# Cached loads and broadcast queries issued by GpSimd, and fourteen matmuls of ones ahead of the first transposition

## The chip, the cores and the metric

The kernel runs on one core of a Trainium2 chip. The metric is the device time of one execution in microseconds. Before the change three runs took 1572.55, 1575.05 and 1578.77 us; their median is 1575.05 us.

The engines are named as the profile names them: PE is TensorE (PEld its weight loads), DVE is VectorE, ACT is ScalarE, POOL is GpSimd, SP is SyncE. SP computes nothing here and issues transfers. "SPq" and "ACTq" are the instructions with which SP and ACT issue them.

## The reference

One inference step of a small decoder with two layers, for a prompt of 512 tokens and for 8 sequences of 8 new tokens each. Layer 0 is attention, layer 1 a state-space layer; each is followed by a gated feed-forward layer. Only the attention of the 8 sequences touches the caches, and the change lies there:

```
DIL_GROUPS = ((128, 1), (512, 4), (2048, 16))        # window, dilation
q = rope(rmsnorm(qkv[:, :, 0], q_gain), pos); k = rope(rmsnorm(qkv[:, :, 1], k_gain), pos); v = qkv[:, :, 2]
for g, (win, dil) in enumerate(DIL_GROUPS):
    kv_all = concatenate([bufs[g], kv_new], axis=1)   # cache, then the new rows
    o, l = dilated_block(q[:, :, g], kv_all, qi, dil, win // dil + 1)
wts = softmax(stack(lses)); o = einsum('gbqh,gbqhd->bqhd', wts, stack(outs))
```

A query of group g sees the cached keys at distances 0, d, 2d, up to the window, 129 keys in each group. The eight new tokens of a sequence together need 1, 4 and 8 sets ("units") of 128 cached rows in the three groups. A unit of keys or of values is 128 rows of 512 fp32 numbers, 256 KB. The caches are also outputs, shifted by 8 rows. All arithmetic is fp32; large matmuls are done as three products of parts rounded to fp32r (`mm6`, and L351 to L353).

## The kernel before

**Order of work.** `_build` (L51) runs in this order: the projections (`qkv_phase`, L417), the attention (`attn_phase`, L596), the output projection (`wo_phase`, L737), the first feed-forward layer with the setup of the state-space layer as filling, the state-space layer, the second feed-forward layer. The Tile framework takes this program with a list of dependences, lets buffers rotate in pools, and puts each engine's instructions into an order with its own model of time (`schedule_with_timeline_sim=True`, L1354). At run time each engine, SP and its transfers included, works through its list in that order and waits where an instruction is not ready.

**The start.** `Tokens.__init__` (L234) issues the first loads: the identity matrix (ACT's queue, L246), the norm gains `gr` (L247 and L253), and in turn a quarter of the prompt `xn` (L250) and a piece of the first weight (L255, by `fetch_w`, L85). The first PE instruction transposes `gr` into a PSUM tile `ps` (L260), and DVE copies the result to `gm` (L261). The prompt's transpositions (`prompt`, L263, PE at L272) are placed after L260 by `issue_after` in `prep` (L311), and their results are scaled by `gm` on ACT (L274). `ones` is a constant of 128x128 that DVE fills at L62; before the change only `Norm.finish` (L196) multiplies with it.

**The projections.** `qkv_chunk` (L330) makes 512 columns of queries, keys or values of one group, 24 prompt and 4 sample matmuls for each of four weight pieces of 512 KB, which ACT and DVE split into `whi` (L99) and `wlo` (L100). The order of the nine chunks is: group 2 (window 2048) queries, keys, values, then queries and keys of groups 1 and 0, then values of groups 1 and 0 last.

**The cached keys** are worked in between. After each weight piece `step` (L502) looks in `PLAN`, a table written by hand, for what is to be traced at this place.
- Groups 1 and 0: `score` (L466). GpSimd clears and fills `Qz` (L471 to L479), `cache_tile` (L385) loads two units of keys into a `kc` buffer, PE transposes them (L488) and multiplies (L492).
- Group 2: `products` (L392). A load of two units of keys (L388) and a load of two queries, broadcast over 128 partitions from a DRAM scratch `qscr` (L396), both into `kc` buffers; they are multiplied (L397) and summed by DVE (L399). For six sequences this happens in the projections with DVE as multiplier and the pool `kst`, for the last two in the attention with GpSimd as multiplier and a pool `kpa` of four buffers. `close2` (L402) ends a sequence; GpSimd clears its `P` (L461 or L726) first.

**The attention.** `attn_phase` runs four head pairs of the prompt (`prompt_pair`, L621; its values `vt` were loaded at L592) and the eight sequences (`decode`, L668), two of them around each pair. A decode loads the new rows' values `vn` (L694) and 13 units of cached values in seven loads by `cache_tile` (L700) into the same `kst` pool of six `kc` buffers, and multiplies them (L704).

**Queues.** All cached loads (L388) and the broadcast queries (L396) are issued by SP, in one list with the weights (L87), the shifted copies of the caches (`pace`, L78, 80 of about 1 MB and 8 of 480 KB), `vn`, `vt` and the rest. ACT's queue has the outputs of new keys and values and the scratch stores. GpSimd issues no transfer.

Of the kernel before, what the change touches and what calls it, by code (L numbers as in the profile page):

```python
# [29 lines left out]
WIN = (128, 512, 2048)  # L30
# [10 lines left out]
def dram(ap, off, dims):  # L41
    return bass.AP(tensor=ap.tensor, offset=ap.offset + off, ap=[list(d) for d in dims])
# [190 lines left out]
class Tokens:  # L233
    def __init__(self, nc, A, L, kst, ptp, small, dk, xr):  # L234
        self.nc, self.L, self.ptp, self.small, self.kst, self.dk, self.xr = nc, L, ptp, small, kst, dk, xr
        c1 = L["c1"]
        self.h = c1.tile([128, KT, T], F32R, name="xh")
        self.l = c1.tile([128, KT, T], F32R, name="xl")
        self.s = c1.tile([128, KT, 128], F32R, name="xsp")
        self.ss = c1.tile([128, 4, 5], F32, name="ss")  # L240
        nc.vector.memset(self.ss, 1.0)
        self.raw, self.mark = [], {}
        ident, gm = L["ident"], L["gm"]
        gr = small.tile([32, 128], F32, name="gr")
        self.w = []
        nc.scalar.dma_start(ident, A["c_ident"])  # L246
        nc.sync.dma_start(gr[0:16], A["norm_mix"].rearrange("l (k p) -> (l k) p", p=128))  # L247
        for i in range(4):
            xn = kst.tile([128, 4, 256], F32, name="kc")
            nc.sync.dma_start(xn, dram(A["x_prompt"], i * 256, [[4 * D, 128], [D, 4], [1, 256]]))  # L250
            self.raw.append(xn)
            if i == 0:
                nc.scalar.dma_start(gr[16:32], A["norm_ffn"].rearrange("l (k p) -> (l k) p", p=128))  # L253
                nc.scalar.activation(self.ss[:, 0, 0:1], self.ss[:, 0, 0:1], AF.Copy)
            self.w.append(L["fetch_w"](A["w_qkv"], 4608, i * 2, 2, 2 * 512, 512, 0.0))  # L255
            if i == 0:
                self.rs = kst.tile([64, D], F32, name="kc")
                nc.sync.dma_start(self.rs, A["x_sample"].rearrange("b j d -> (b j) d"))
        ps = L["psd"].tile([128, 136], F32, name="Sd")
        self.first = nc.tensor.transpose(ps[:, :32], gr, ident[:32, :32])  # L260
        self.gmc = nc.vector.tensor_copy(gm.rearrange("p (l m) k -> p m l k", m=2), ps[:, :32].rearrange("p (m l k) -> p m l k", m=2, l=2))  # L261

# [117 lines left out]
CACHES = ("cache_kv_w128", "cache_kv_w512", "cache_kv_w2048")  # L380
# [4 lines left out]
def cache_tile(nc, A, pool_, name, gi, b, c0, n, kv):  # L385
    t = pool_.tile([128, 2, 512], F32, name=name)[:, :n]
    st = STRIDE[gi]
    nc.sync.dma_start(t, dram(A[CACHES[gi]], (b * WIN[gi] + c0) * 1024 + kv * 512, [[st * 1024, 128], [1024, n], [1, 512]]))  # L388
    return t


def products(nc, A, L, eng, kst, P, b, part):  # L392
    c0 = 2 * part
    kc = cache_tile(nc, A, kst, "kc", 2, b, c0, 2, 0)
    qb = kst.tile([128, 2, 512], F32, name="kc")
    nc.sync.dma_start(qb, dram(L["qscr"], (b * 8 + c0) * 512, [[0, 128], [512, 2], [1, 512]]))  # L396
    eng.tensor_tensor(kc, kc, qb, OP.mult)  # L397
    for c in range(2):
        nc.vector.tensor_reduce(P[:, :, 0:2, c0 + c], kc[:, c].rearrange("p (a h d) -> p a h d", a=4, h=2), AX.X, OP.add)  # L399
# [17 lines left out]
def qkv_phase(nc, tc, A, es, L):  # L417
# [40 lines left out]
    def score2(b, part):  # L458
        if part == 0:
            prods[b] = dk.tile([128, 4, 4, 8], F32, name="P2", bufs=1)  # L460
            g.memset(prods[b], 0.0)  # L461
        products(nc, A, L, v, kst, prods[b], b, part)
        if part == 3:
            close2(nc, L, dk, psd, "Sd", prods.pop(b), b)

    def score(gi, b):  # L466
# [14 lines left out]
        for c0 in range(0, n, 2):  # L481
            w = min(2, n - c0)
            kc = cache_tile(nc, A, kst, "kc", gi, b, c0, w, 0)
            for c in range(w):
                u = c0 + c
                kp = ptp.tile([128, 4, 128], F32, name="pt")
                for hp in range(4):
                    te.transpose(kp[:, hp, :], kc[:, c, hp * 128:(hp + 1) * 128], ident)  # L488
                ks = dk.tile([128, 4, 128], F32, name="ks")
                s.activation(ks, kp, AF.Copy)  # L490
                for hp in range(4):
                    te.matmul(Sd[hp * 32:hp * 32 + 32, 0:128], Q[:, u, hp, :], ks[:, hp, :], start=u == 0, stop=u == n - 1,  # L492
                              tile_position=(0, hp * 32), skip_group_check=True)
# [102 lines left out]
def attn_phase(nc, tc, A, es, L):  # L596
# [71 lines left out]
    def decode(b):  # L668
# [28 lines left out]
        for gi in (0, 1, 2):  # L697
            for c0 in range(0, UNITS[gi], 2):
                w = min(2, UNITS[gi] - c0)
                vc = cache_tile(nc, A, kst, "kc", gi, b, c0, w, 1)  # L700
                for c in range(w):
                    for hp in range(4):
                        pz = pa[:, hp, :] if u == 0 else Z[:, u - 1, hp, :]
                        te.matmul(O[hp * 32:hp * 32 + 32, :], pz, vc[:, c, hp * 128:hp * 128 + 128], start=u == 0, stop=False, tile_position=(0, hp * 32), skip_group_check=True)  # L704
                    u += 1
# [14 lines left out]
    def score2():  # L720
        if not rest:
            return
        b, part = rest.pop(0)
        if part == 0:
            prods[b] = dk.tile([128, 4, 4, 8], F32, name="P2", bufs=1)
            g.memset(prods[b], 0.0)  # L726
        products(nc, A, L, g, kp, prods[b], b, part)
        if part == 3:
            close2(nc, L, dk, pD, "Sd", prods.pop(b), b)
# [628 lines left out]
```

## Time and profile before

| | |
|---|---|
| median of three runs | 1575.05 us |
| the profiled execution's own time | 1576.93 us |
| its span, first to last instruction | 1575.1 us |
| mean granted clock of PE | 0.978 |
| busy: PE, DVE, ACT, POOL | 1518.4, 925.1, 519.2, 304.1 us |
| cached loads, issued by SP | 96 of 512 KB, 16 of 256 KB |
| broadcast queries, issued by SP | 32 of 512 KB |
| moved by SP's queue | 304.81 MB |
| moved by ACT's queue | 18.04 MB |

The views used below are: the page with the busy time of each engine; the busy time by stretch (columns: from and to in us, length, then for each engine busy us and number of instructions, the granted clock of PE as a share of full speed, the mean busy share of the 16 DMA engines, and GB/s); the waits (who waited for whom: us in total, times, longest); and the order of time (start, duration, engine, line, operation, tiles written and read, and in brackets how long the engine stood before it and what released it). A row with x4 joins four instructions that follow each other. A view of one source line gives shortest, median and longest duration in ns. The chain of waits goes back from the last instruction to what released it.

The projections last until about 303 us, the attention until 463, the output projection starts at 465; from 480 us on the feed-forward and state-space layers follow.

### The profile page before, as it was taken

The page shows a single profiled execution, that of the slowest core. Times are in us where ns is not written, and L with a number is a line of the kernel's source. Part 1 is how long each engine was busy: PE and PEld are TensorE (multiplying, and loading weights), DVE is VectorE, ACT ScalarE, POOL GpSimd, SP SyncE. Part 2 cuts the span into 40 slices and gives each one's busy share as a digit, 9 for nine tenths or more (in the row PEclk, how much of TensorE's full clock was granted, in tenths as well). Part 3 has the DMA queues.
Part 4 walks back from the last instruction along what each step waited for, and adds up shares of the span by engine and source line. Part 5 has one row for each costly group of instructions (what it writes and reads, how often), then busy time and mean ns, then how long its engine had stood idle before and what let it go on. Part 6 is the DMA issues. An engine that isn't in the chain of part 4 may idle for free.

```text
span 1575.1 us, 28895 instructions
## 1 busy us (share of the span) xinstructions
PE 1518.4 (96%) x12010; PEld 1404.5 (89%) x12010; DVE 925.1 (59%) x1665; ACT 519.2 (33%) x774; POOL 304.1 (19%) x339
## 2 busy tenths in 40 slices
PE   8989999769989999999999999999999999999998
PEld 6868877546669999999999999999999999999998
DVE  5898954458637864388879667755353333333332
ACT  4433444424425222222222254333242212221222
POOL 2000111213003013745335430021011001100100
PEclk9999999879999999999999999899999999999999
DMA  8496248896786656589666765855555555443212
GB/s 274 164 345 216 98 132 273 285 346 232 250 281 169 224 187 220 186 293 315 212 236 241 242 225 180 273 163 195 189 186 203 209 186 212 144 142 95 81 61 81
DMA packets 193219, 324.69 MB, mean 206 GB/s; under 512 B 39488, under 2 KB 137024, under 8 KB 191552
## 3 DMA queue, kind: packets, MB, share of 16 engines
q1 hardware_dynamic: 183584, 304.81, 56.7%
q10 hardware_dynamic: 9504, 18.04, 3.3%
q8 instruction: 94, 1.54, 0.4%
q14 instruction: 37, 0.30, 0.1%
HBM read 290.27 MB, written 119.83 MB: 260 GB/s over the span
## 4 chain that ended last, share of the span: by engine, by line
PE 52%; DVE 2%; DMA 1%; issue 0%; ACT 0%; ACTq 0%; DVEq 0%
PE acc L106 48%; DMA u_scr<-uP 1%; PE aux L106 1%; DVE cb L1052 1%; DVE kk L1061 1%; PE acc L1180 0%; PE acc L1181 0%; PE acc L1142 0%; PE aux L1181 0%; PE aux L1045 0%; PE aux L1180 0%; DMA U<-u_scr 0%; PE aux L1056 0%; DVE Z L1162 0%; PE aux L818 0%
## 5 line engine op out<-in xcount | busy, mean ns | idle before, releaser
L100 DVE TENSOR_TENSOR wlo<-raw,whi 128x1024 fp32r<-128x1024 f32 x200 | 246.3, 1232 | 263.0 <-ACT whi L99 256.5
L99 ACT ACTIVATE whi<-raw 128x1024 fp32r<-128x1024 f32 x200 | 208.4, 1042 | 518.9 <-PE acc L106 403.1
L106 PE MATMUL acc<-xgl,whi 128*128 128x288 f32 x1760 | 378.6, 296 | 0.0
L106 PE MATMUL acc<-xgh,wlo 128*128 128x288 f32 x1760 | 377.7, 296 | 0.0
L106 PE MATMUL acc<-xgh,whi 128*128 128x288 f32 x1760 | 377.0, 296 | 0.1
L106 PEld LDWEIGHTS acc<-xgl,whi 128*128 128x128 f32 x1760 | 282.6, 188 | 1.2 <-issue 1.0
L106 PEld LDWEIGHTS acc<-xgh,wlo 128*128 128x128 f32 x1760 | 282.7, 188 | 0.6 <-issue 0.2
L106 PEld LDWEIGHTS acc<-xgh,whi 128*128 128x128 f32 x1760 | 281.7, 188 | 0.5 <-DVE gt L795 0.3
L797 POOL TENSOR_TENSOR gt<-gt,rstd 128x576 f32<-128x576 f32 x44 | 77.2, 1755 | 431.4 <-ACT gt L796 431.3
L106 PE MATMUL acc<-hh,whi 128*128 128x288 f32 x704 | 151.4, 296 | 0.0
L106 PE MATMUL acc<-hh,wlo 128*128 128x288 f32 x704 | 151.3, 296 | 0.0
L106 PE MATMUL acc<-hl,whi 128*128 128x288 f32 x704 | 151.1, 295 | 0.0
L352 PE MATMUL acc<-wlo,xh 128*128 128x512 f32 x288 | 114.4, 398 | 4.9 <-DVE wlo L100 4.8
L106 PEld LDWEIGHTS acc<-hh,wlo 128*128 128x128 f32 x704 | 113.1, 188 | 0.2 <-issue 0.2
L106 PEld LDWEIGHTS acc<-hl,whi 128*128 128x128 f32 x704 | 113.1, 188 | 0.2 <-issue 0.2
L106 PEld LDWEIGHTS acc<-hh,whi 128*128 128x128 f32 x704 | 113.2, 188 | 0.0
L353 PE MATMUL acc<-whi,xl 128*128 128x512 f32 x288 | 110.5, 394 | 0.0
L351 PE MATMUL acc<-whi,xh 128*128 128x512 f32 x288 | 106.7, 402 | 1.0 <-ACT whi L99 0.9
L191 POOL TENSOR_TENSOR ssum<-ssum,sq 128x576 f32<-128x576 f32 x21 | 36.0, 1714 | 209.9 <-ACT sq L190 209.9
L352 PEld LDWEIGHTS acc<-wlo,xh 128*128 128x128 f32 x288 | 54.7, 190 | 16.6 <-DVE wlo L100 5.9
L351 PEld LDWEIGHTS acc<-whi,xh 128*128 128x128 f32 x288 | 54.7, 191 | 13.2 <-ACT whi L99 1.3
L809 DVE TENSOR_TENSOR xT<-acc,xT 128x576 f32<-128x576 f32 x48 | 36.2, 755 | 49.2 <-PE acc L106 49.2
(350 smaller groups left out, 2037.3 us busy)
## 6 DMA issues: line engine op xcount, KB each, us to landing
o_kv_s<-cache_kv_w SPq DMA_DIRECT2D x64, 1020.0 KB
kc<-cache_kv_w SPq DMA_DIRECT2D x96, 512.0 KB
raw<-ffn_w_gate SPq DMA_DIRECT2D x44, 512.0 KB
raw<-ffn_w_up SPq DMA_DIRECT2D x44, 512.0 KB
raw<-ffn_w_down SPq DMA_DIRECT2D x40, 512.0 KB
raw<-w_qkv SPq DMA_DIRECT2D x36, 512.0 KB
kc<-qscr SPq DMA_DIRECT2D x32, 512.0 KB
o_kv_s<-cache_kv_w SPq DMA_DIRECT2D x16, 1008.0 KB
```

The source lines that it names most:

```text
L99: s.activation(hi, raw, AF.Copy)
L100: mark[0] = v.tensor_tensor(lo, raw, hi.bitcast(F32), OP.subtract)
L106: te.matmul(ps[:, c, :HN], w, x[:, c * HN:(c + 1) * HN], start=first and i == 0, stop=last and i == 2)
L191: g.tensor_tensor(self.ss, self.ss, sq, OP.add)
L351: te.matmul(ps[t], ah, wh[:, k2, :], start=k == 0, stop=False)
L352: te.matmul(ps[t], ah, wl[:, k2, :], start=False, stop=False)
L353: te.matmul(ps[t], al, wh[:, k2, :], start=False, stop=k == KT - 1)
L797: g.tensor_tensor(t, t, nin.r, OP.mult)
L809: v.tensor_tensor(xv, ps[m][:, :, :HN], xv, OP.add)
L1052: v.tensor_copy(cb[i][hs, :, gl, :], c[hs, qs, :])
L1061: v.scalar_tensor_tensor(k7, dmask, dcol[:, f:f + 1], k7, op0=OP.mult, op1=OP.add)
```

## The change

Three places. The fourteen matmuls multiply `ones` by `ones` into the tile that the first transposition overwrites; nothing reads what they write. The two transfers get another issuing engine; their buffers and readers stay.

```diff
         ps = L["psd"].tile([128, 136], F32, name="Sd")
+        for _ in range(14):
+            nc.tensor.matmul(ps[:, :128], L["ones"], L["ones"], start=True, stop=True)
         self.first = nc.tensor.transpose(ps[:, :32], gr, ident[:32, :32])
...
 def cache_tile(nc, A, pool_, name, gi, b, c0, n, kv):
     t = pool_.tile([128, 2, 512], F32, name=name)[:, :n]
     st = STRIDE[gi]
-    nc.sync.dma_start(t, dram(A[CACHES[gi]], (b * WIN[gi] + c0) * 1024 + kv * 512, [[st * 1024, 128], [1024, n], [1, 512]]))
+    nc.gpsimd.dma_start(t, dram(A[CACHES[gi]], (b * WIN[gi] + c0) * 1024 + kv * 512, [[st * 1024, 128], [1024, n], [1, 512]]))
     return t
...
     qb = kst.tile([128, 2, 512], F32, name="kc")
-    nc.sync.dma_start(qb, dram(L["qscr"], (b * 8 + c0) * 512, [[0, 128], [512, 2], [1, 512]]))
+    nc.gpsimd.dma_start(qb, dram(L["qscr"], (b * 8 + c0) * 512, [[0, 128], [512, 2], [1, 512]]))
     eng.tensor_tensor(kc, kc, qb, OP.mult)
```

## The prediction

> **What bounds the kernel now.** I read the page's busy times first, then the busy times by stretch, then the waits of PE and of SP, then the order of time where PE waits.
>
> ```profile
> span 1575.1 us, 28895 instructions
> PE 1518.4 (96%) x12010; PEld 1404.5 (89%) x12010; DVE 925.1 (59%) x1665; ACT 519.2 (33%) x774; POOL 304.1 (19%) x339
> ```
>
> ```profile
> core 0: us, PE busy (x) PEld busy (x) DVE busy (x) ACT busy (x) POOL busy (x), PEclk, DMA share, GB/s
> 160.00:200.00 40.00, 40.00 (x186) 32.88 (x186) 37.62 (x67) 18.20 (x29) 4.85 (x12) 1.00 0.32 109
> 280.00:320.00 40.00, 25.26 (x259) 18.69 (x258) 18.28 (x46) 16.13 (x26) 11.14 (x39) 0.80 0.84 301
> 800.00:1200.00 400.00, 396.98 (x3159) 392.76 (x3158) 250.74 (x356) 142.93 (x209) 86.67 (x68) 0.97 0.63 213
> ```
>
> PE is busy 96% of the span. From 480 us on it has no room at all (396.98 of 400 in one stretch), and nothing the change touches runs there. What can be won lies before: at the start, in 280 to 360 (the last cache scores and the first decode), and in 440 to 463 (the last values). In 280 to 320 PE is busy 25.26 of 40 us and the granted clock is down to 0.80.
>
> ```profile
> PE pt L488 <- DMA kc<-cache_kv_w: 12.6, 2, 10.8
> PE acc L352 <- DVE wlo L100: 4.8, 2, 2.9
> PE Sd L704 <- DMA kc<-cache_kv_w: 4.7, 6, 1.2
> ```
>
> PE's waits for cached loads come to 12.6 + 4.7 = 17.3 us in all, and one wait of 10.8 us is most of it.
>
> **The loads.** 112 cached loads and 32 broadcast queries, 144 issues, leave SP's queue for GpSimd's. SP keeps the weights, `vn`, `vt` and the copies of the caches.
>
> ```profile
> L388 SPq DMA_DIRECT2D kc<-cache_kv_w x112: 327/372/1764, 19.3 to 455.7; - x112
> L396 SPq DMA_DIRECT2D kc<-qscr x32: 325/339/722, 66.2 to 383.5; - x32
> SPq L694 <- DMA kc<-cache_kv_w: 4.7, 6, 1.2
> 304.71 0.63 SPq L83 DMA_DIRECT2D o_kv_s<-cache_kv_w  x1
> 306.04 1.63 SPq L592 DMA_DIRECT2D vt<-vtscr  x2
> 310.31 0.39 SPq L388 DMA_DIRECT2D kc<-cache_kv_w  x1
> 318.34 4.45 SPq L388 DMA_DIRECT2D kc<-cache_kv_w  x3
> 324.40 1.97 PE L488 MATMUL pt<-ident,kc 128*128 128x128 f32 x8 [10.78 <-DMA kc<-cache_kv_w]
> ```
>
> The `vn` loads of L694 share no tile with `kc`, yet SP waits six times for a cached load before it issues one. So a queue's transfers wait for older transfers of other tiles. This makes the 10.78 us readable: ahead of the loads that PE wants stand a 1 MB copy and two 1 MB `vt` loads, and the load that ends the wait is issued only at 318.34. On another queue the cached loads no longer stand behind these 3 MB. But the DMA engines are full there, and they are idle a little later:
>
> ```profile
> 315.00:320.00 5.00, 0.00 (x0) 0.00 (x0) 0.00 (x0) 0.00 (x0) 0.00 (x0) 0.50 1.05 379
> 325.00:330.00 5.00, 2.75 (x39) 2.24 (x37) 2.16 (x6) 1.19 (x2) 1.23 (x6) 0.50 0.87 275
> 330.00:335.00 5.00, 3.97 (x41) 2.73 (x45) 2.37 (x7) 1.20 (x2) 0.00 (x0) 0.50 0.94 313
> 360.00:370.00 10.00, 9.10 (x55) 5.45 (x56) 8.79 (x27) 3.17 (x9) 2.81 (x2) 0.66 0.19 57
> ```
>
> At 315 to 320 no engine computes and the DMA share is 1.05 at 379 GB/s. Bytes do not get faster by being issued elsewhere; only their order changes. The 3 MB are 3.1 MB / 379 GB/s = 8.3 us; if two queues share the engines evenly, half of that comes after the wanted loads instead of before: **-4 us**. The bounds are 0 (the values of the first decode, right behind, wait for the same bytes) and the whole 17.3 us plus what the clock of 0.50 costs in 325 to 335, half of 2.75 + 3.97, that is 3.4 us: -20.7. I stay near the small end because of the 379 GB/s. When the stall shrinks, the values of the first decode are late next, then `vt`, whose loads now share.
>
> [...]
>
> **Earlier, in the projections (66 to 290),** PE waits 4.8 us for `wlo`, and DVE, which makes it, works in order and stands at products that wait for their queries:
>
> ```profile
> DVE kc L397 <- DMA kc<-qscr: 21.8, 12, 7.2
> ```
>
> There DMA has room (share 0.32 in 160 to 200), and the loads are held by the six `kc` buffers, which don't change. I take **-1 us** (bounds -4.8 and +3, if a load behind a waiting GpSimd instruction comes late).
>
> **GpSimd's queue.** It was empty of DMAs; now 144 issues stand in line with its own work, and it waits in order:
>
> ```profile
> POOL Qz L471 <- PE Sd L495: 129.4, 14, 53.5
> POOL kc L397 <- DMA kc<-qscr: 31.2, 7, 9.2
> 302.23 0.45 POOL L479 COPY Qz<-att 64x32 f32<-64x32 f32 x2
> 294.03 1.35 POOL L479 COPY Qz<-att 64x32 f32<-64x32 f32 x2
> 294.04 1.27 DVE L100 TENSOR_TENSOR wlo<-raw,whi 128x1024 fp32r<-128x1024 f32 x1
> 358.11 2.35 POOL L397 TENSOR_TENSOR kc<-kc 128x1024 f32<-128x1024 f32 x1 [6.77 <-DMA kc<-qscr]
> ```
>
> Behind a memset of `Qz` or `P` that waits for PE, and behind a product of L397 that waits for its query (31.2 us in all), stand cached loads, the values of later decodes among them; the first broadcast also waits there for the store of `qscr` (L555, still SP's). No row prices a DMA issued by GpSimd. Bounds: 0.33 us, SP's fastest, and 2.35 us, GpSimd's own instruction over such a tile. I take 0.4 to 1 us, nearest to SP's median of 0.372, since the transfer is the same one. What hides it is the transfer itself:
>
> ```profile
> 440.00:450.00 10.00, 8.52 (x133) 5.83 (x133) 5.22 (x24) 3.72 (x12) 0.00 (x0) 1.00 0.98 347
> 445.53 5.61 SPq L388 DMA_DIRECT2D kc<-cache_kv_w  x6
> 461.29 1.08 PE L704 MATMUL Sd<-kc,Pz 128*32 128x128 f32 x16 [0.65 <-DMA kc<-cache_kv_w]
> ```
>
> A decode's values are 13 units of 256 KB, 3.25 MB in 7 loads, 3.4 MB / 347 GB/s = 9.8 us, or 1.4 us a load. As long as an issue costs less, GpSimd keeps ahead. There remains the later first landing of a batch, some 0.6 us (1 less 0.4) in each of the last two batches, where PE waits for each load as it comes: **+1 us**; from -2 to +6 with products in front.
>
> **The matmuls of ones.** 14 fp32 matmuls of 128x128 on 128 columns stand ahead of L260.
>
> ```profile
> 0.86 0.17 DVE L62 MEMSET ones<- 128x128 f32 x1
> 3.19 0.28 PE L260 MATMUL Sd<-ident,gr 32*128 32x32 f32 x1 [3.19 <-DMA gr<-norm_ffn]
> 5.17 1.97 PE L272 MATMUL pt<-ident,kc 128*128 128x128 f32 x8 [1.70 <-DMA kc<-x_prompt]
> 8.08 2.08 PE L351 MATMUL acc<-whi,xh 128*128 128x512 f32 x4 [0.94 <-ACT whi L99]
> 14.70 0.40 PE L353 MATMUL acc<-whi,xl 128*128 128x512 f32 x1
> 21.79 1.07 PE L353 MATMUL acc<-whi,xl 128*128 128x512 f32 x4
> 1012.65 0.43 PE aux L1181 x2
> 949.01 0.97 PE aux L196 x4
> ```
>
> The same four matmuls take 2.08 us at 8 us and 1.07 us at 21 us, a factor of 1.94; the fall comes by 14.70, 6.6 us after the first. An fp32 matmul with a 128x128 weight takes two instructions, 0.43 us with 72 columns and 0.97/2 = 0.49 us with 288; at the slow clock 0.43 x 1.94 = 0.83. Ones are ready at 1.03. With about 6 us of slow clock, 7 matmuls take 6 us and the other 7 take 3 us: L260 starts at 10.0 instead of 3.19. From the prompt's transpositions to the first large matmul it was 8.08 - 5.17 = 2.9 us, less half of the 1.97 - 0.8 that the faster clock saves; the first large matmul comes at about 12.4, 4.3 us late. In return the matmuls of 8.08 to 14.70 run at full clock and give 6.6 x 0.48 = 3.2 us back. Net **+1 us**. Bounds: at the 0.25 us of the slow transpositions all 14 take 3.5 us (-2); all at 0.49 x 1.94 they take 13.3 us (+5). Nothing covers this: from 15 us on the projections' matmuls follow each other without a gap.
>
> **Sum.** -4 - 1 + 1 + 1 = -3 us on the profiled execution of 1576.9 us (span 1575.1), which lies 1.9 us above the median of 1575.05. On the median: **1572 us**.
>
> **Rivals.**
> A, *the stall goes whole.* The wait at 313 to 324 was one of order: the wanted loads go out as soon as buffers are free, PE stays warm. Then -20.7 + 1 = -20, 1555 us. For it: the load that ended the wait went out 8 us after the one of 310.31. Against: 379 GB/s while nothing computes, and decode values next in line.
> B, *GpSimd's issue becomes the bound* (the slower side). It decides from 1.4 us an issue. At 1.9 us seven issues take 13.3 us, 3.5 over the transfer; for the six batches from 380 on that is +21, 1594 us; at 2.35 it is 6 x 6.6 = +40, 1613. For it: the copy of 1.35 us that takes 0.45 elsewhere lay beside a DVE product, so DVE delays GpSimd by 0.9 us, and DVE is busy 37.6 of 40 us in places. 0.4 + 0.9 = 1.3 is just under the point. Against: many DVE instructions there read PSUM. [...]
> C, *the loads move nothing:* the bytes bind, and only the ones' delay stays: +1 to +5, 1576 to 1580 us.
>
> **How the numbers follow.** A measurement of this kernel tells 0.5% (7.9 us) from no change: faster is under 1567, slower over 1583. Forecast 0.45 (of it 0.04 under, 0.03 over), A 0.22, B 0.23, C 0.10. So faster 0.26, same 0.48, slower 0.26. The forecast's own range is 1564 to 1585; to leave out no more than 2 in 10 I go to A's 1555 and to the middle of B: 1555 to 1596.
>
> **What would show it.** Right: L260 at 8 to 12 us, no matmul of 0.63 us after it; PE's wait at L488 of some 6 us instead of 10.8; DMA share still near 1 in 300 to 350; GpSimd's issues at a median under 1.4 us. Wrong: values waiting behind GpSimd's products, PE waits at L704 well above 4.7 us, DVE instructions longer beside GpSimd's issues, or wo_phase starting over 10 us away from 465.

## The result, and the profile after

The changed kernel takes 1597.55 us in the median of four runs (1594.33 to 1599.08), the kernel before 1576.91 us in the median of its four (1572.55 to 1580.81). The ratio is 1.0129 with a 95% interval of 1.0096 to 1.0162: the change made the kernel 15 to 26 us slower. No change was forecast, 1572 us, and the result lies just above the range's end of 1596.

The profiled execution of the changed kernel took 1599.08 us. In its lines everything behind L258 stands two lines lower: the cached load is L390, the broadcast query L398, the transposition of keys L490, the product of values L706. The page's head, the busy times by stretch and the waits, as they were shown of before:

```profile
span 1597.3 us, 28968 instructions
PE 1534.7 (96%) x12038; PEld 1409.4 (88%) x12038; DVE 928.5 (58%) x1665; ACT 518.8 (32%) x774; POOL 403.0 (25%) x483
```

```profile
core 0: us, PE busy (x) PEld busy (x) DVE busy (x) ACT busy (x) POOL busy (x), PEclk, DMA share, GB/s
160.00:200.00 40.00, 39.32 (x186) 31.32 (x185) 36.34 (x62) 21.76 (x37) 6.46 (x12) 1.00 0.33 97
280.00:320.00 40.00, 29.29 (x266) 21.70 (x264) 16.52 (x40) 16.36 (x26) 18.38 (x47) 0.82 0.80 271
800.00:1200.00 400.00, 394.93 (x3213) 389.58 (x3214) 263.31 (x386) 141.87 (x207) 94.78 (x73) 1.00 0.65 218
```

```profile
PE pt L490 <- DMA kc<-cache_kv_w: 10.1, 3, 6.5
PE Sd L706 <- DMA kc<-cache_kv_w: 7.4, 11, 2.8
PE acc L354 <- DVE wlo L100: 4.7, 1, 4.7
```

None of these lines holds 20 us. PE's waits for cached loads are 10.1 + 7.4 = 17.5 us in all, as before (17.3), and the longest fell from 10.8 to 6.5. The price of an issue by GpSimd is now a row (shortest, median and longest in ns, then first and last start):

```profile
L390 POOL DMA_DIRECT2D kc<-cache_kv_w x112: 537/712/880, 16.5 to 481.3; - x112
L398 POOL DMA_DIRECT2D kc<-qscr x32: 547/574/623, 70.5 to 393.3; - x32
```

The loss shows when the stages are compared in order of time. The last products of decode 0 and of decode 1 and the first matmul of the output projection, before:

```profile
344.68 0.42 PE L707 MATMUL Sd<-vn,pn 24*32 24x128 f32 x8
...
384.12 0.42 PE L707 MATMUL Sd<-vn,pn 24*32 24x128 f32 x8
...
465.20 1.09 PE L106 MATMUL acc<-ath,whi 128*128 128x288 f32 x3 [1.32 <-ACT ath L746]
```

and after:

```profile
351.91 0.42 PE L709 MATMUL Sd<-vn,pn 24*32 24x128 f32 x8
...
405.43 0.42 PE L709 MATMUL Sd<-vn,pn 24*32 24x128 f32 x8
...
492.45 1.81 PE L106 MATMUL acc<-ath,whi 128*128 128x288 f32 x6 [1.32 <-ACT ath L748]
```

Decode 0 ends 7.2 us later, decode 1 21.3, the attention 27.3, and the span is 22.2 us longer: 7 us were lost up to the first decode, 14 in the first head pair, which lies between the two decodes, 6 in the rest of the attention, and 5 came back behind it. The largest part, the first head pair, comes first. The same stretch of both kernels, before and then after (PE's granted clock is the third number from the end):

```profile
345.00:400.00 55.00, 53.41 (x629) 33.89 (x625) 47.27 (x152) 24.30 (x65) 19.61 (x12) 0.94 0.76 271
```

```profile
345.00:400.00 55.00, 48.66 (x368) 27.43 (x370) 36.34 (x100) 13.97 (x39) 32.45 (x34) 0.61 0.70 240
360.00:370.00 10.00, 6.72 (x39) 3.70 (x38) 6.91 (x19) 2.28 (x6) 5.19 (x6) 0.52 0.78 261
370.00:380.00 10.00, 10.00 (x52) 6.05 (x51) 7.80 (x24) 4.24 (x12) 6.87 (x7) 0.50 0.61 193
380.00:390.00 10.00, 10.00 (x49) 4.97 (x48) 9.03 (x19) 2.14 (x9) 5.85 (x8) 0.50 0.40 127
```

PE does 368 instructions in 55 us where it did 629, at a clock of 0.61 instead of 0.94. From 370 to 390 it is shown as fully busy and yet has about 50 instructions in 10 us: the clock stands at half. How it came to that is seen in the order of time on PE. Before (S are the scores of the first head pair, L635 to L642, which stand among the products of values of decode 0, L704; part of the order of time):

```profile
338.81 0.71 PE L642 MATMUL S<-kT,qT 64*128 64x128 f32 x8
...
340.02 0.65 PE L704 MATMUL Sd<-kc,Pz 128*32 128x128 f32 x16
340.59 0.62 PE L635 MATMUL S<-kT,att 64*32 64x256 f32 x2
341.14 0.71 PE L642 MATMUL S<-kT,qT 64*128 64x128 f32 x4
341.78 0.64 PE L704 MATMUL Sd<-kc,Pz 128*32 128x128 f32 x16
...
345.57 1.09 PE L651 MATMUL pt<-ident,sm 128*128 128x128 f32 x8
```

After:

```profile
350.67 1.31 PE L706 MATMUL Sd<-kc,Pz 128*32 128x128 f32 x32
351.91 0.42 PE L709 MATMUL Sd<-vn,pn 24*32 24x128 f32 x8
352.26 0.71 PE L644 MATMUL S<-kT,qT 64*128 64x128 f32 x8
...
359.06 0.65 PE L653 MATMUL pt<-ident,sm 128*128 128x128 f32 x4 [1.06 <-DVE sm L621]
359.64 0.71 PE L644 MATMUL S<-kT,qT 64*128 64x128 f32 x4
363.63 0.63 PE L640 MATMUL S<-kT,att 64*32 64x256 f32 x1 [3.28 <-DVE mx L649]
```

Before, the first quarter's scores were finished (338.81) while decode 0 was still multiplying, DVE made their softmax beside it, and the transpositions of the result followed without a gap at 345.57. After, the planner put the last scores of the first quarter behind decode 0 (352.26); PE then runs out of scores, waits 1.06 and 3.28 us for the softmax, and at 360 the clock falls. Before, it falls at 362 too, but is back at 369. DVE in that gap:

```profile
357.19 1.81 DVE L621 TENSOR_SCALAR sm<-sm,rd 128x512 f32<-128x512 f32 x1
358.93 1.27 DVE L401 TENSOR_REDUCE P<-kc 128x8 f32<-128x512 f32 x2
360.11 0.15 DVE L620 RECIPROCAL rd<-den 128x1 f32<-128x1 f32 x1
360.30 1.36 DVE L621 TENSOR_SCALAR sm<-sm,rd 128x512 f32<-128x512 f32 x1
361.58 1.27 DVE L401 TENSOR_REDUCE P<-kc 128x8 f32<-128x512 f32 x2
362.88 0.69 DVE L649 CUSTOM_DVE_ANT_0 sm<-S,mp 128x512 f32<-128x512 f32 x1
```

So the first theory: **the loss is in the instruction lists.** With the loads on GpSimd the planner (which orders each engine's list by its own model) lists the first head pair differently, and PE falls to half clock. Rivals: GpSimd's loads themselves, whatever the list; or the matmuls of ones.

### The profile page after: what moved, and what is told of

Read it like the earlier page. It is cut to its first block, busy times and chain, and to the rows that moved or that the text cites. A ratio compares the mean times of both kernels' runs of the same rounds, so it can differ in the third digit from the quotient of the medians.

```text
span 1597.3 us, 28968 instructions
## 1 busy us (share of the span) xinstructions
PE 1534.7 (96%) x12038; PEld 1409.4 (88%) x12038; DVE 928.5 (58%) x1665; ACT 518.8 (32%) x774; POOL 403.0 (25%) x483
## 5 line engine op out<-in xcount | busy, mean ns | idle before, releaser
L100 DVE TENSOR_TENSOR wlo<-raw,whi 128x1024 fp32r<-128x1024 f32 x200 | 246.6, 1233 | 255.1 <-ACT whi L99 251.5
L390 POOL DMA_DIRECT2D kc<-cache_kv_w x112 | 77.6, 694 | 183.9 <-PE pt L490 56.6
```

The costliest lines, as they stand in the source:

```text
L100: mark[0] = v.tensor_tensor(lo, raw, hi.bitcast(F32), OP.subtract)
L390: nc.gpsimd.dma_start(t, dram(A[CACHES[gi]], (b * WIN[gi] + c0) * 1024 + kv * 512, [[st * 1024, 128], [1024, n], [1, 512]]))
```

## The experiments

Each kernel is compared with runs of before on the same chip; a loss in us is the ratio less one, times 1575 us. The extra matmuls of some kernels write tiles that are overwritten before they are read.

**Parts of the change alone.** Ones alone:

```diff
+        for _ in range(14):
+            nc.tensor.matmul(ps[:, :128], L["ones"], L["ones"], start=True, stop=True)
         self.first = nc.tensor.transpose(ps[:, :32], gr, ident[:32, :32])
```

> The kernel before with the fourteen matmuls of ones alone; all transfers stay on SP. Theory 1 (the loss is made where the loads of the attention changed their queue, in the first head pair): the trace of the changed kernel lost about 4 us of its 22 in the first chunk, so this kernel is 2 to 5 us slower than before, with the first transposition near 6.5 us instead of 3.2, the second chunk's first matmul near 44 instead of 40, and everything behind it only shifted by that. Theory 2 (the matmuls of ones change the list of the whole kernel or the clock's record, and the attention pays for it): 15 to 22 us slower, with the long stretch of half clock in the first head pair. Theory 3 (the start costs nothing in the end, what it loses is taken up by a later wait for transfers): within 1.5 us of before.

Measured: 1.0014 (0.9994 to 1.0033), +2.2 us. The second theory of that text is out; the interval does not tell the first (2 to 5 us) from the third (within 1.5). In its trace the output projection starts 9.5 us late and the span is only 1.7 us longer; how this comes back is told at the end.

Both loads on GpSimd, no ones (the diff of the change without its first part):

> The changed kernel without the matmuls of ones: both loads issued by GpSimd everywhere. Theory 1 (queue in the attention): 15 to 18 us slower than before, that is the changed kernel less its 4 us of the start; the first head pair again stretched to about 50 us at half the clock. Theory 2 (ones): within 5 us of before. Theory 3 (the start is given back later): as slow as the changed kernel, 19 to 22 us above before.

Measured: 1.0066 (1.0040 to 1.0091), +10.4 us, between what the second theory said (within 5) and what the first said (15 to 18). Here the planner kept the scores among decode 0's products, but in the profile decode 0 itself ends 6.3 us later than before, with the clock at half from 306 to 353 us (before: 308 to 338). The parts, 2.2 and 10.4 us, make 12.6 and not 20.3; with the three intervals the difference of 7.7 us has about 7 to either side.

Only the projections' loads on GpSimd:

```diff
-    nc.sync.dma_start(t, ...
+    (nc.gpsimd if kv == 0 and pool_.name == "kst" else nc.sync).dma_start(t, ...
-    nc.sync.dma_start(qb, ...
+    (nc.gpsimd if kst.name == "kst" else nc.sync).dma_start(qb, ...
```

> Only the loads of the projections (cached keys and broadcast queries into the pool kst) are issued by GpSimd; in the attention the loads of values, keys and queries stay on SP. Theory 1 (the loss comes from the attention's loads on GpSimd's queue): 0 to 5 us slower than before, the projections end about 3 us later and the first head pair is as before. Rival (the list of the projections as rearranged shifts the work so that the first head pair falls into half clock, whoever issues its loads): 12 to 20 us slower, with the clock near 0.5 from about 355 to 395 us.

Measured: 0.9985 (0.9960 to 1.0009), -2.4 us, no difference that can be told. Decode 0 ends at 345.4 us, where it ended at 344.8, and PE's waits for cached keys come to 12.6 us in all, as before. And only the attention's loads (the two engines exchanged):

> The other half: SP issues in the projections, GpSimd issues the values of the decodes, and the keys and queries of the last two sequences. Theory 1: the projections end where they did before (the last transposition of keys at about 332 us), decode 0 too, and then the first head pair loses 15 to 23 us; the time is 12 to 20 us above before. Rival (the projections' order makes the loss): within 4 us of before.

Measured: 1.0110 (1.0080 to 1.0140), +17.3 us. The projections are cleared, the attention carries it. There, the values alone (`nc.gpsimd if kv else nc.sync` in `cache_tile`):

> Only the loads of the decodes' values are issued by GpSimd; keys and queries stay on SP everywhere, no matmuls of ones. In PE's list this kernel, like the one with all loads of the attention on GpSimd, has the last scores of the first head pair's first quarter behind decode 0's last product instead of among its products. Theory 1 (that place in the list makes the loss): 12 to 20 us slower than before, with the clock at 0.5 over most of 355 to 395 us. Rival (GpSimd's products of keys and queries behind the loads in its queue make the loss, so their transfers must be on it too): within 6 us of before.

Measured: 1.0107 (1.0081 to 1.0133), +16.9 us. And the keys and queries of the last two sequences alone (`nc.gpsimd if pool_.name == "kpa" else nc.sync`, and the same for `qb`):

> Only the keys and queries of the last two sequences (the pool kpa) are issued by GpSimd, between its own products; values stay on SP. PE's list of decode 0 and the first quarter is that of before. Theory 1 (place in the list): within 4 us of before, the half clock of the first head pair no longer than the 7 us of before. Rival (GpSimd's loads and products hold each other and DVE up): 10 to 20 us slower.

Measured: 1.0036 (1.0008 to 1.0063), +5.7 us. Neither theory of that text said this (within 4, or 10 to 20), and the mean hides two groups: seven of the ten runs took 1575 to 1582 us at a mean clock of 0.978 to 0.983, three took 1589 to 1592 at 0.972 to 0.974. So the decodes' values on GpSimd are enough for nearly the whole loss. In the list of the kernel with the values alone part of the first quarter's scores stands behind decode 0, and PE waits 7.74 us for a softmax there.

**The list without the loads.** The kernel before with four score matmuls put behind decode 0's last product, nothing else in the program (`behind` is that product; it orders PE's list and adds no wait):

```diff
+            with (tc.issue_after(behind.ins) if behind is not None and r == 0 else ExitStack()):
                 for gi in (1, 2):
                     ...
```

> The kernel before, every transfer on its old queue and no matmuls of ones; only in PE's list the last four score matmuls of the first quarter of the first head pair are placed behind decode 0's last product of values, where the slower kernels have them. Nothing waits on it but the list. Theory 1 (the list makes the loss): 10 to 18 us slower than before, with PE short of work around 350 us and then a long stretch at half clock in the first head pair. Rival (GpSimd's issue and transfers make the loss, the list is no more than its sign): within 5 us of before.

Measured: 1.0065 (1.0041 to 1.0088), +10.2 us, the clock at 0.50 from 350 to 384 us. The edit names four matmuls, but the planner ordered the rest anew around them: read from the traces, PE's order differs from before's in 43 places, DVE's in 30 and ACT's in 19, all behind 338 us. So another list, with every load on SP, is enough to bring the half clock; that these four matmuls alone do it is not shown. The other way round, the changed kernel with the first quarter's scores traced and listed ahead of decode 0's products:

```diff
+        ready = scores(hp, 0) if hp == 0 else None
-        decode(2 * hp)
+        decode(2 * hp, ready[1] if ready else None)
...
+                with (tc.issue_after(behind.ins) if behind is not None else ExitStack()):
                     for c in range(w):
```

> The changed kernel whole, loads on GpSimd and matmuls of ones, but the scores of the first quarter of the first head pair are traced and listed ahead of decode 0's products, so that their softmax runs beside them. Theory 1 (list): it gains back most of what the first head pair lost, 10 to 18 us of the changed kernel's 20.6, and the time is 3 to 10 us above before; the half clock after 355 us is gone or below 10 us. Rival (GpSimd's issue, or DVE held by GpSimd's products): it stays 15 us or more above before.

Measured: 1.0072 (1.0049 to 1.0095), +11.3 us. It gains back 9 us of the 20.3 (about 6 to either side), just under what was said for the list; the rest stays. Its profile is of the fastest of the four runs (1584.04 us; the others took 1589 to 1591): there the half clock in 350 to 400 us is down to 10 us from 38.

**List and issuer told apart.** All instructions of PE, DVE and ACT can be pinned in another kernel's order by an edge from each to the one before it:

```diff
+def pin_lists(nc, tc):
+    traced = list(nc.cur_bb.bb.instructions)
+    for blob in LISTS.values():
+        at = ...  # the order, as numbers of traced instructions
+        for a, b in zip(at[:-1], at[1:]):
+            tc.add_manual_dep(traced[b], traced[a].name, ...NoSync...)
```

The traces show that it held: in the five pinned kernels the three engines run their instructions in the order of the kernel named, apart from the ones. GpSimd's loads, no ones, with the lists of before:

> All cached loads and broadcast queries issued by GpSimd, no matmuls of ones, but the lists of PE, DVE and ACT are pinned, instruction for instruction, to those of the kernel before; only SP's and GpSimd's lists are new. Without the pins this kernel took 9.7 us more than before. Theory 1 (the lists make the loss): within 4 us of before, and the first head pair's half clock is about the 7 us of before. Rival (GpSimd's issue, its transfers, or its hold on DVE make it): 7 to 15 us slower, now with waits for kc at the products of values or at DVE that the lists of before do not have.

Measured: 1.0170 (1.0128 to 1.0213), +26.8 us. **Here the first theory fell**: with the old lists GpSimd's loads cost not nothing but more than twice the 10.4 us of the planner's own list; the rival's 7 to 15 us were too few as well. In its profile the clock stands at half without a break from 312 to 391 us, and decode 0 ends 11.8 us late: here a part of the loss lies ahead of the first head pair, at the cached keys and decode 0. The reverse, every load on SP, with the lists of the kernel that has its values on GpSimd:

> The reverse: every transfer is issued by SP as before, no matmuls of ones, but the lists of PE, DVE and ACT are pinned to those that the kernel with GpSimd's loads of values had, which was 16.9 us slower than before. Theory 1 (the lists make the loss): 10 to 20 us slower, with a clock of 0.5 from about 350 to 395 us. Rival (who issues makes it): within 5 us of before.

Measured: 1.0100 (1.0066 to 1.0135), +15.8 us, about what GpSimd's values cost with the same lists (16.9). The stretch of 345 to 400 us in this kernel, in which GpSimd issues nothing:

```profile
345.00:400.00 55.00, 50.58 (x374) 31.02 (x373) 34.54 (x105) 16.18 (x41) 19.69 (x12) 0.57 0.59 204
```

374 instructions at a clock of 0.57: the changed kernel's picture without its loads. Both are true, then. GpSimd's loads cost under the old list, and the list that the planner makes for the values on GpSimd costs whoever issues. The changed kernel's own lists with every load on SP were not run. The changed kernel with the lists of before behind its ones:

> The changed kernel whole, with the matmuls of ones first in PE's list and GpSimd's loads, and behind the ones the lists of PE, DVE and ACT of the kernel before. Theory 1 (lists): 0 to 5 us slower than before instead of 20.6. Rival (ones and GpSimd's loads together make the loss, whatever the list): 15 to 22 us slower.

Measured: 1.0233 (1.0211 to 1.0254), +36.7 us, twice the loss of the change. Both theories missed it. It is near the sum of what the loads (26.8, above) and the ones (6.9, below) cost under these lists.

**What GpSimd's loads do under the old list.** The values alone on GpSimd, lists of before:

> Only the values of the decodes are issued by GpSimd, no matmuls of ones, and the lists of PE, DVE and ACT are pinned to those of before. Theory B (values issued by GpSimd land later than the list of before allows, PE waits for them and falls to half clock): 10 to 25 us slower, with waits of the products of values for the cache loads in decode 0 well above before's. Theory A' (the list alone: who issues the values does not matter): within 5 us of before.

Measured: 1.0122 (1.0097 to 1.0148), +19.2 us, as theory B said; the values on GpSimd are enough, without any new list on the other three engines. The long wait came in decode 1 and not in decode 0. GpSimd's order of time shows how it came, then PE's:

```profile
389.44 2.35 POOL L397 TENSOR_TENSOR kc<-kc 128x1024 f32<-128x1024 f32 x1 [3.15 <-DMA kc<-qscr]
391.73 4.16 POOL L388 DMA_DIRECT2D kc<-cache_kv_w  x6
```

```profile
384.88 2.37 PE L704 MATMUL Sd<-kc,Pz 128*32 128x128 f32 x80
390.08 0.55 PE L651 MATMUL pt<-ident,sm 128*128 128x128 f32 x3
397.77 1.08 PE L704 MATMUL Sd<-kc,Pz 128*32 128x128 f32 x16 [7.14 <-DMA kc<-cache_kv_w]
```

The buffers that the next values go into come free while PE multiplies what is in them, from 384.88 to 387.25. But six loads of values stand in GpSimd's list behind one of its own products, which waits 3.15 us for its query and takes 2.35. They go out together from 391.73, 4.5 us after the last of PE's products; PE waits 7.14 us for the first of them, and the clock is at 0.50 from 392 to 416. In the kernel before SP issues the six loads while the same products still run:

```profile
378.73 2.37 PE L704 MATMUL Sd<-kc,Pz 128*32 128x128 f32 x80
379.91 3.52 SPq L388 DMA_DIRECT2D kc<-cache_kv_w  x6
```

This explains one stall. The clock was also at half from 358 to 375 us, ahead of it, and that it too comes from late values is not shown.

**Is it the waits or the clock?** The listed variant above (+10.2 us) with eight matmuls of ones of 128x512 more in the first head pair, to give PE work where it would wait:

```diff
+            if hp == 0 and r in (1, 2, 3):
+                for h in (0, 1, 0, 1) if r == 1 else (0, 1):
+                    te.matmul(S2[h], L["ones"], kT[0][:, hp, :T], start=True, stop=True)
             for b in range(4):
```

> The kernel with SP's queue and the four score matmuls listed behind decode 0 (10.2 us slower than before), with extra PE work in the first head pair: eight matmuls of ones by the keys, 128x512 each, ahead of the scores of quarters 1 to 3 (four, two, two), into the score tiles that the scores then overwrite. Theory 1a (PE's low activity there lets the clock fall, and the fall carries the loss): the clock stays near 1.0 in 350 to 385 us although PE has some 7 us more to do, and the time is equal to or below that kernel's, 3 to 9 us above before. Rival 1b (the waits of the softmax chain carry it and the clock only follows): the eight matmuls add their own time, 13 to 20 us above before, or the clock stays at 0.5 all the same.

Measured: 1.0032 (1.0012 to 1.0052), +5.0 us. More work did not make the kernel slower, but some 5 us faster (with about 5 to either side); the clock in 345 to 385 us is 0.94 where it was 0.57. That is as theory 1a said. But the planner ordered PE, DVE and ACT anew here too (PE's order differs in 22 places), so a part may be the list's; and the profile is of the fastest of ten runs that took 1573 to 1586 us. The same eight matmuls in the changed kernel:

> The changed kernel whole, with eight more matmuls of ones (128x512, ahead of the scores of quarters 1 to 3 of the first head pair, overwritten by them), some 7 us of PE work more. Theory A (half clock carries the loss of the changed kernel): the stretch at 0.5 from 360 to 398 us is gone or below 15 us, and the time falls to 4 to 13 us above before in spite of the added work. Theory B (late values carry it, the clock only follows): the time stays at 18 us or more above before, and the added matmuls come on top.

Measured: 1.0113 (1.0089 to 1.0138), +17.8 us. The half clock went as theory A said, but the time came out between the two, next to B's 18. The stretch in the changed kernel, then in this one, and from the groups of instructions the eight matmuls of this one (two instructions each; busy us, mean ns):

```profile
360.00:398.00 38.00, 34.72 (x183) 19.12 (x185) 28.28 (x80) 10.28 (x29) 22.25 (x23) 0.51 0.60 191
```

```profile
360.00:398.00 38.00, 35.15 (x351) 22.05 (x353) 29.50 (x93) 13.30 (x38) 25.08 (x25) 0.87 0.57 182
```

```profile
L633 PE MATMUL S<-kT,ones 128*128 128x512 f32 x16 | 8.1, 618 | 0.0
```

PE does 351 instructions instead of 183 in the same 38 us, with the clock at 0.87 instead of 0.51. Over all its runs the kernel spends 31 us less at half clock than the changed kernel does, worth up to 15 us; the added work takes up to 8.1 us of that back, which leaves 7, and 2.5 were measured, with about 6 to either side.

The two kernels with the eight matmuls, compared with each other, say more. In both profiles the clock falls in 350 to 400 us for no longer than 7 and 10 us (before: 7). From the end of decode 0 to the output projection the one with all loads on SP takes 122.7 us, near the 120.4 of before; the changed one takes 137.8. So with the same added work and hardly more half clock, GpSimd's loads and the ones, with the lists that go with them, still cost the attention some 15 us. Over all runs the two kernels lose 5.0 and 17.8 us, with 5 and 12 us more at half clock than before. So this part is not carried by the half clock.

The same pair of kernels warns of reading a stage from one profile: up to the end of decode 0 the changed kernel and the one with eight matmuls more have the same order on PE, DVE, ACT and GpSimd, and yet decode 0 ends at 352.1 us in one profile and at 346.0 in the other. So the 7 us lost up to the first decode are not shown to belong to the change.

The ones with the lists of before, all loads on SP:

> The matmuls of ones alone, all transfers on SP, with the lists of PE, DVE and ACT of before behind the ones. Without the pins the second chunk started 4 us late. If the ones cost by their own time on PE: again 4 us late at the second chunk. If it was the list that came with them: 1.5 us late or less, and the time within 4 us of before.

Measured: 1.0044 (1.0021 to 1.0067), +6.9 us. The second chunk starts 0.7 us late instead of 4: over 3 of those 4 us were the list's. The time missed what was said. In this profile the first head pair is at half clock from 358 to 375 us, where before is for 7 us; but the ones with the planner's list, whose order from 110 us on is before's too, have only 7 us in 350 to 400, so this may be chance. The two losses of the ones, 2.2 and 6.9 us, can't be told apart with their intervals.

**All kernels together.** Each run's mean granted clock is known. If it takes only the values 1 and 0.5, as the stretches show it, a run of t us at a mean clock c spent 2 x (1 - c) x t us at half clock, and loses at most half of that. Before's runs spent 58 us so (mean clock 0.9815).

| kernel | loss, us | more half clock than before, us | half of it |
|---|---|---|---|
| the change | 20.3 | 42 | 21 |
| ones | 2.2 | 0 | 0 |
| both loads | 10.4 | 15 | 7 |
| projections' loads | -2.4 | -6 | -3 |
| attention's loads | 17.3 | 32 | 16 |
| values | 16.9 | 41 | 20 |
| keys and queries, last two | 5.7 | 9 | 4 |
| four scores later, SP | 10.2 | 29 | 14 |
| same, with eight matmuls | 5.0 | 5 | 2 |
| values' lists, SP | 15.8 | 33 | 17 |
| change, scores first | 11.3 | 30 | 15 |
| change, with eight matmuls | 17.8 | 12 | 6 |
| both loads, lists of before | 26.8 | 39 | 20 |
| change, lists of before | 36.7 | 51 | 25 |
| values, lists of before | 19.2 | 20 | 10 |
| ones, lists of before | 6.9 | 9 | 4 |

The last column is the most that the half clock can cost. For the change it just reaches the loss. A lower price can be read from runs of one kernel, which have the same lists and differ by chance: over the 150 runs of all kernels, each compared with the mean of its own set, 1 us more at half clock goes with 0.32 us more of time (0.28 to 0.36). By this price the 42 us are worth some 14 of the 20.3 us. That is an estimate from a correlation: a wait can lengthen both. The kernels that lost clearly more than the last column were given work (the eight matmuls) or kept the old lists.

## Why the prediction was wrong

**The step that failed** is in "GpSimd's queue": "As long as an issue costs less, GpSimd keeps ahead. There remains the later first landing of a batch, some 0.6 us ... in each of the last two batches ... +1 us; from -2 to +6 with products in front." The price was right: 0.712 us in the median for a cached load, 0.574 for a query, within the 0.4 to 1 us taken and half of the 1.4 at which it was to decide. But this term of +1 us, for the attention's loads in GpSimd's list, measures 17.3 us, 16.9 of them with the values alone. Two things were not in it. First, the durations and waits were added up on the lists of before, though the part ahead of the prediction says that the planner orders each engine's list with its own model of time: the list that it makes for the values on GpSimd costs 15.8 us with all loads on SP. Second, a wait of PE of a few us was priced at its own length: under the lists of before the values alone cost 19.2 us, with one wait of 7.14. In the first head pair such waits stand next to a half clock that lasts: 38 us at 0.51 in the changed kernel. By the two prices above, the half clock of the whole kernel is worth some 14 to 21 of the 20.3 us. That the clock matters there stood in the prediction's own rows (0.80 in 280 to 320, 0.66 in 360 to 370), but it entered only as 3.4 us of the stall's upper bound.

**The stall at the transposition of keys** was forecast to fall from 10.8 to some 6 us; its longest wait is 6.5 us, though three waits together still make 10.1, against 12.6. The DMA engines moved no more in these stretches than they had: up to 396 GB/s at a share of 1.08 before (300 to 310 us), up to 395 at 1.04 after (320 to 325). The -4 us of this term arrived nowhere: in no profile with these loads on GpSimd does decode 0 end earlier than before.

**The projections**, forecast -1 us: -2.4 with the interval reaching over zero. The wait for `wlo` is 4.7 us in the changed kernel, as it was, but 2.7 us with the projections' loads alone on GpSimd: a gain of 2 us in the waits, which in the time lies within the noise.

**The ones**, forecast +1 (-2 to +5): +2.2 alone. The steps behind the number were too slow:

```profile
1.09 5.48 PE L261 MATMUL Sd<-ones 128*128 128x128 f32 x28 [1.09 <-DVE ss L241]
6.51 0.24 PE L262 MATMUL Sd<-ident,gr 32*128 32x32 f32 x1
6.68 1.09 PE L274 MATMUL pt<-ident,kc 128*128 128x128 f32 x8
8.74 1.20 PE L353 MATMUL acc<-whi,xh 128*128 128x512 f32 x4 [0.97 <-ACT xh L276]
...
20.26 0.63 PE L358 MATMUL acc<-whi,xsp 128*128 128x512 f32 x1
```

The 14 matmuls take 5.48 us, 0.39 each (two instructions), where the forecast had 0.43 for half of them and 0.83 for the others; so the first transposition starts at 6.51 us, not 10. The first large matmul is 0.7 us late (8.74 against 8.08) and not 4.3. The full pace came early, as forecast: eight transpositions take 1.09 us where they took 1.97, and the trace's record of the clock begins, at 1.0, at 5.5 us where it began at 14.2. That the first matmuls are slow by the clock was the author's estimate from their durations (2.08 us against 1.07); ahead of these two times no clock is recorded. But the clock fell once more, to 0.5 from 19.2 to 22.6 us, which the forecast had ruled out ("no matmul of 0.63 us after it").

**Rival B** gave 1594 us, near the 1597.55 measured, but by luck and not by its mechanism: no issue took more than 0.88 us. (Its own sum is about 1 us off: 1572 and 21 make 1593.) A busy DVE did not hold the issues up: the 18 of cached loads that ran beside DVE's L621 took 0.722 us in the median and 0.789 at most, against 0.712 and 0.880 for all cached loads. What B took its 0.9 us from, instructions of DVE and GpSimd that last longer beside each other, is seen here too: the L621 of 1.81 us above takes 0.49 us elsewhere and lay beside a product of GpSimd from 356.37 to 358.72. Not every pair shows it: in the profile of before the two copies of `Qz` at 294.03 took 1.35 us beside L100, against 0.45 at 302.23, while the copy at 243.26 took 0.20 beside L497, which reads PSUM. None of this is part of the change, since such products of GpSimd stood in the kernel before too. **Rival A** did not come: the stall's longest wait shrank by 4 us and did not go. **Rival C** (the loads move nothing, the ones cost 1 to 5 us) fits the ones alone (+2.2) and the projections' loads alone (-2.4); the attention's loads are what it left out.

Of the signs named for a wrong forecast, two came in the changed kernel: the output projection starts 27 us from 465, and PE waits 7.4 us at the product of values. Values that wait behind GpSimd's products were shown only under the old lists. DVE's instructions were not longer beside GpSimd's issues: `wlo` took 1.22 us both beside them and alone.

**What came back.** Behind the attention the profiled execution of before loses time that the changed one doesn't. Before, then after:

```profile
1000.00:1050.00 50.00, 48.35 (x419) 47.37 (x419) 32.56 (x60) 19.27 (x46) 10.39 (x19) 0.80 0.70 210
```

```profile
1000.00:1050.00 50.00, 49.02 (x549) 47.50 (x549) 41.27 (x76) 21.64 (x56) 0.56 (x5) 1.00 0.90 282
```

A mean clock of 0.80 over 50 us is 20 us at half speed, up to 10 us of loss, in the state-space layer. None of the sixteen other profiles has it in this stretch. Whether all executions of before have it can't be said from one profile.

**Open.** Why the clock stays down for 38 us while PE is shown as busy. What the half clock carries of the change's loss: some 14 to 21 us by the prices above, while the two kernels with eight matmuls leave some 15 us in the attention without it; together that is more than was lost, so one of the two is too high. How much of the values' lateness is the issue (0.71 us against SP's 0.37) and how much their place behind GpSimd's own work; in the changed kernel itself PE's waits for values stay at 2.8 us and below. Values on GpSimd with its products on another engine were not tried. Of all versions the projections' loads on GpSimd came out lowest (0.9985, interval over 1); none beats before by more than can be told.

## What to carry to other kernels

A transfer that moves to another queue also moves the planner's order on engines that have nothing to do with it: compare the lists of the two kernels around every stage where one engine waits for another, before adding up durations of the old list. Where PE works in short matmuls that wait for a softmax, price a wait of a few microseconds not by its length alone but also by the half clock that may follow in that stage (here 37.5 us of it, beside waits of 1.06 and 3.28 us), and read the granted clock of each stage first. Loads that another engine needs don't belong in the list of an engine whose own instructions wait for transfers: six loads of values went out 4.5 us after the products that freed their buffers, because a product that waited for its query stood in front of them. And where an edit lets the planner order everything anew, pin the lists before calling the edit the cause.

## What the runs showed of the hardware

The half clock outlasts the wait. In the changed kernel PE waits 3.28 us for the softmax up to 363.63 us, and the clock is recorded at 0.5 from 360.5 to 398.0: 0.51 over the 38 us from 360 to 398, in which the profile shows PE busy for 34.72 us. It came back at 398.0 us, when the products of the next decode had begun (396.95). In the kernel with eight matmuls of 128x512 more and lists of its own the same stretch had 0.87, with PE busy for 35.15 us. What in the work keeps the clock down is not shown.

With the lists pinned the parts of the change add up within their intervals: the loads 26.8 us and the ones 6.9, together 33.7, and 36.7 measured. With the planner's own lists they hardly do (12.6 and 20.3).

GpSimd's issue of a 512 KB or 256 KB load takes 0.712 us of its time in the median, SP's 0.372. A busy DVE did not lengthen it: of all 144 issues in the changed kernel those beside a DVE that was busy for over 80% of the time took 0.707 us in the median (0.789 at most), as did those beside one that was busy for under 20% (0.707).
